# Expert slots of a fused encoder kernel laid out by token block, scattered once per two expert pairs

## The chip, the cores and the metric

The kernel runs on one core of a Trainium2 chip. The metric is the device time of one execution in microseconds (us); it is the median of three runs. The engines are named as in the profile: PE is TensorE (matmuls), PEld its weight loads, DVE is VectorE, ACT is ScalarE, POOL is GpSimd, and SP issues the DMAs.

## The reference, cut to what matters

Two layers work on x of 256 tokens by 1024 features, all in float32. Each layer has a token mixer and then a mixture of experts. The change touches the mixture of experts alone:

```
gate = one_hot(group) * (g_val * w_inner)         # (256 tokens, 16 experts), two nonzero in a row
hg = einsum('td,edf->tef', h, w_gate)             # w_gate, w_up: 16 x 1024 x 256
hu = einsum('td,edf->tef', h, w_up)
act = silu(hg) * hu * gate[..., None]
y = einsum('tef,efd->td', act, w_down)            # w_down: 16 x 256 x 1024
x = x + gt_f * y
```

The kernel doesn't compute all 256 x 16 products. Each expert has slots for the tokens that chose it: 32 (`CAP`) for each of the two blocks of 128 tokens. What does not fit goes through a loop, `extra`, which with these inputs runs for one pair of experts only (layer 1, pair 4).

## The kernel before, in words

The kernel writes out the order of the instructions of each engine by hand: they stand in program order, and an engine works strictly in that order. In each layer the experts are done in eight pairs, p = 0 to 7. One pair holds two experts of 64 slots, so 128 slots are the 128 partitions of every tile of that pair: 64 of the first expert (32 of block 0, 32 of block 1), then 64 of the second.

A pair goes through these steps:

- `gate_up` (L891): x of the slots (`xeT`) by the gate and up weights (`wgu`) gives `pgu`, 128 slots by 512. Two experts run side by side, each on 64 columns of the PE array, eight steps of the contraction, float32.
- `extra(p)` (L948): a branch on a counter; when it is zero, each engine jumps over the loop.
- `activate`: ACT takes the silu of the gate half (L906), DVE multiplies it with the up half and with `gs`, the gate weight of each slot (L907).
- `slots` for the next pair: POOL has written the selection matrix weighted by the gate (`sg`, L853); PE turns it (`pst`, two transposes, L897), ACT sums each row to `gs` (`junk`, L899, with an accumulator read behind it), DVE makes the 0/1 matrix `ST` (L901).
- for p < 4, `gather` of a part of x for the pairs 4 to 7: PE writes `pg` (L875), ACT (L881) and DVE (L883) scale it into `xeT`.
- half of `scatter` of the pair before (L942): `ST` by the two parts of its result (`yhi`, `ylo`), added to y in PSUM, token block 0; four matmuls.
- `turn`: PE transposes the activation (`pat`, L913), DVE copies it to SBUF (`atT`, L915).
- the other half of `scatter`, token block 1.
- `down` (L924): `pd`, two halves n of 512 features; behind each, DVE multiplies with the modulation (`yw`, L928), ACT rounds to `yhi` (L930), DVE takes the rest `ylo` (L932).

Pair 7 has no `slots`, and its result is scattered behind the loop (L1048 to L1051): the half n = 0 as yhi and ylo, the half n = 1 unsplit in float32 (`yw`). After it come the residual copies and the next layer, or in layer 1 the last norm and the store.

DMAs of weights are issued by SP up to two pairs ahead. Their order is the same in both kernels.

Of the kernel before, what the change touches and what calls it, by code (L numbers as in the profile page):

```python
# [7 lines left out]
F32 = mybir.dt.float32  # L8
F32R = mybir.dt.float32r
# [3 lines left out]
AF = mybir.ActivationFunctionType  # L13
# [4 lines left out]
P = 128  # L18
# [32 lines left out]
def encoder(ctx: ExitStack, tc: tile.TileContext, a: dict, out: bass.AP, dbg=None):  # L51
# [12 lines left out]
    def mid(name, shape=(P, D), dt=F32):  # L64
        return w4.tile(list(shape), dt, name=name, tag="w4")
# [49 lines left out]
    G.memset(ones, 1.0)  # L115
    zeros = const.tile([P, 1], BF16, name="zeros")
    G.memset(zeros, 0.0)
    sg = [const.tile([P, NB, 2, SL], F32, name=f"sg{i}") for i in range(2)]
    for t in sg:
        G.memset(t, 0.0)  # L120
# [632 lines left out]
    def experts(l):  # L753
# [140 lines left out]
        def slots(src, t=None):  # L894
# [6 lines left out]
            V.tensor_scalar(st, t, 0.0, None, op0=OP.is_gt)  # L901
            return gs_, st

        def activate(gate, up, gs_):
# [13 lines left out]
        def down(p, at, ts=(None, None), Y=None, last=False):
            hi, lo, w = Y or (mid("yhi", dt=F32R), mid("ylo", dt=F32R), mid("yw"))
            for n in range(2):  # L920
                t = bank("pd") if ts[n] is None else ts[n]
                for f in range(2):
                    for e in range(2):
                        mm(t[e * SL:(e + 1) * SL, :], at[:, f, e * SL:(e + 1) * SL],  # L924
                           WTS[l, p][2, e][:, f, n * 512:(n + 1) * 512], start=(f == 0), stop=(f == 1),
                           skip_group_check=True)
                sl = slice(n * 512, (n + 1) * 512)
                V.tensor_tensor(w[:, sl], t, gt[l, 1][:, sl], op=OP.mult)  # L928
                if not last or n == 0:
                    S.activation(hi[:, sl], w[:, sl], AF.Copy)  # L930
                if not last:
                    V.tensor_tensor(lo[:, sl], w[:, sl], hi[:, sl].bitcast(F32), op=OP.subtract)  # L932
            if last:
                sl = slice(0, 512)
                V.tensor_tensor(lo[:, sl], w[:, sl], hi[:, sl].bitcast(F32), op=OP.subtract)
            return hi, lo, w

        def scatter(st, Y, first, last, bs=(0, 1), ns=(0, 1)):
            for b in bs:
                for xi in range(2):  # L940
                    for n in ns:
                        mm(y[b][:, n * 512:(n + 1) * 512], st[:, b * P:(b + 1) * P],  # L942
                           Y[xi][:, n * 512:(n + 1) * 512], start=(first and xi == 0),
                           stop=(last and xi == 1), skip_group_check=True)

        def extra(p):
            v = nc.values_load(nx[0:1, p:p + 1], min_val=0, max_val=3)
            with tc.If(v > 0):  # L948
                rx = sm.tile([P, NB, 2], F32, name="rx", bufs=1)
                V.tensor_copy(rx, rk[:, :, 2 * p:2 * p + 2])  # L950
                with tc.For_i(0, v, 1):
                    V.tensor_scalar_add(rx, rx, -float(CAP))
                    gx = small("gx", (P, NB, 2, SL))
                    for b in range(NB):
                        V.tensor_tensor(sx[:, b, :, b * CAP:(b + 1) * CAP], iota[:, None, :].to_broadcast([P, 2, CAP]),
                                        rx[:, b, :, None].to_broadcast([P, 2, CAP]), op=OP.is_equal)
# [4 lines left out]
                    xr = mid("xr")  # L961
# [11 lines left out]
                    Y = mid("yhi", dt=F32R), mid("ylo", dt=F32R), mid("yw")  # L973
                    xe = Y[2].rearrange("p (d s) -> p d s", d=DC)
# [70 lines left out]
        st, Y = prev  # L1045
        for b in range(NB):
            s = st[:, b * P:(b + 1) * P]
            mm(y[b][:, 0:512], s, Y[0][:, 0:512], start=False, stop=False, skip_group_check=True)  # L1048
            mm(y[b][:, 512:D], s.bitcast(F32), Y[2][:, 512:D], start=False, stop=True,  # L1049
               skip_group_check=True)  # L1050
            mm(y[b][:, 0:512], s, Y[1][:, 0:512], start=False, stop=True, skip_group_check=True)  # L1051
# [110 lines left out]
```

## Time and profile before

| | before |
|---|---|
| median of 3 runs (lowest to highest) | 619.03 us (618.54 to 619.41) |
| the profiled execution's own time | 620.14 us |
| span of the profile, first to last instruction | 618.3 us |
| PE busy | 570.4 us, 92% of the span |
| DVE busy | 348.8 us, 56% |
| ACT busy | 212.5 us, 34% |
| mean granted clock of PE | 0.988 of full speed |

Busy shares are averages over the whole kernel. PE does little else than matmuls in the expert stages, from 179 to 298 us in layer 0 and from 477 to 610 us in layer 1; what the other engines set there are the short stretches between the end of a pair's `gate_up` and the start of its `down`. "Issue" as a releaser means that the engine waited for nothing that the profile shows.

### The profile page before, as it was taken

To read this page: it belongs to the slowest core of one execution; us is meant where nothing else is said; L and a number is where in the kernel's file an instruction comes from. 1 tells how busy PE (TensorE), PEld (TensorE's weight loads), DVE (VectorE), ACT (ScalarE), POOL (GpSimd) and SP (SyncE) were. 2 spreads that over 40 slices of the span, in tenths; PEclk is the share of its full clock that TensorE was granted. 3 is DMA by queue.
4 is the path that set the end of the run, shared out by engine and by line. 5 is a ranking of instruction groups with operands and counts; after the bars stand their busy time and mean duration, and the time that the engine had idled before them with its cause. 6 is when DMAs were issued, how large, how long until landed. Compare 5 with 4: busy or idle time off the path is not lost. (4 is left out here: it accounts for less than half of the span.)

```text
span 618.3 us, 8151 instructions
## 1 busy us (share of the span) xinstructions
PE 570.4 (92%) x3010; PEld 353.5 (57%) x3010; DVE 348.8 (56%) x670; ACT 212.5 (34%) x359; POOL 18.3 (3%) x56
## 2 busy tenths in 40 slices
PE   6998999999988999999899989999996999989994
PEld 4666874566444444343577789998864343453341
DVE  3988776542752333232788998899367233324223
ACT  6334345551433111111543744544335111112112
POOL 1000000000010000000000010000001000000000
PEclk9999999999997999999999989999999999999998
DMA  8999869999845999999998738698632799946911
GB/s 327 423 419 420 353 244 391 419 368 420 338 156 216 364 404 418 418 415 420 421 421 355 308 118 317 211 346 344 271 137 72 301 394 408 408 192 238 418 64 68
DMA packets 29188, 197.01 MB, mean 319 GB/s; under 512 B 3328, under 2 KB 3968, under 8 KB 7616
## 3 DMA queue, kind: packets, MB, share of 16 engines
q1 hardware_dynamic: 28832, 195.61, 79.3%
q8 instruction: 38, 0.62, 0.4%
q10 hardware_dynamic: 288, 0.52, 0.2%
q14 instruction: 30, 0.25, 0.1%
HBM read 195.08 MB, written 1.05 MB: 317 GB/s over the span
## 5 line engine op out<-in xcount | busy, mean ns | idle before, releaser
L891 PE MATMUL pgu<-wgu,xeT 128*64 128x512 f32 x512 | 112.7, 592 | 0.0
L891 PEld LDWEIGHTS pgu<-wgu,xeT 128*64 128x64 f32 x512 | 36.6, 137 | 72.3 <-issue 71.7
L219 DVE SCALAR_TENSOR_TENSOR wada<-wada,cact 128x1024 f32<-128x1024 f32 x56 | 66.2, 1218 | 0.7 <-ACT cact L168 0.7
L924 PE MATMUL pd<-wdn,atT 128*64 128x512 f32 x256 | 59.9, 611 | 1.7 <-DVE atT L915 1.7
L930 ACT ACTIVATE yhi<-yw 128x512 fp32r<-128x512 f32 x32 | 20.1, 629 | 94.1 <-DVE yw L928 94.1
L907 DVE SCALAR_TENSOR_TENSOR silu<-pgu,gs,silu 128x256 f32<-128x256 f32 x16 | 7.7, 484 | 75.4 <-ACT silu L906 75.4
L928 DVE TENSOR_TENSOR yw<-pd,gt 128x512 f32<-128x512 f32 x32 | 22.0, 688 | 41.2 <-PE pd L924 41.2
L714 PE MATMUL pu<-hhi,wlo 128*128 128x256 f32 x128 | 37.1, 290 | 2.3 <-DVE wlo L296 2.3
L924 PEld LDWEIGHTS pd<-wdn,atT 128*64 128x64 f32 x256 | 17.4, 140 | 35.8 <-issue 28.8
L714 PE MATMUL pu<-hhi,whi 128*128 128x256 f32 x128 | 37.8, 296 | 0.0
L714 PE MATMUL pu<-hlo,whi 128*128 128x256 f32 x128 | 36.8, 288 | 0.0
L932 DVE TENSOR_TENSOR ylo<-yw,yhi 128x512 fp32r<-128x512 f32 x30 | 20.8, 692 | 21.5 <-ACT yhi L930 13.9
L906 ACT ACTIVATE silu<-pgu 128x256 f32<-128x256 f32 x16 | 6.1, 384 | 74.3 <-PE pgu L891 72.3
L296 DVE TENSOR_TENSOR wlo<-win,whi 128x1024 fp32r<-128x1024 f32 x25 | 30.2, 1220 | 0.6 <-ACT whi L295 0.5
L714 PEld LDWEIGHTS pu<-hhi,wlo 128*128 128x128 f32 x128 | 25.2, 197 | 2.6 <-DVE wlo L296 2.5
L286 ACT ACTIVATE hhi<-hj,B 128x256 fp32r<-128x256 f32 x16 | 8.1, 509 | 52.6 <-DVE hj L278 26.3
L295 ACT ACTIVATE whi<-win 128x1024 fp32r<-128x1024 f32 x25 | 25.7, 1052 | 1.1 <-PE pu L714 1.1
L714 PEld LDWEIGHTS pu<-hhi,whi 128*128 128x128 f32 x128 | 25.3, 197 | 0.0
L714 PEld LDWEIGHTS pu<-hlo,whi 128*128 128x128 f32 x128 | 25.2, 197 | 0.0
L296 DVE TENSOR_TENSOR wlo<-bwo,whi 128x1024 fp32r<-128x1024 f32 x16 | 19.4, 1222 | 7.8 <-ACT whi L295 6.5
L942 PE MATMUL y<-yhi,ST 128*128 128x512 f32 x60 | 21.4, 430 | 0.6 <-PEq L948 0.3
L201 PE MATMUL pada<-wada,cz 128*32 128x512 f32 x160 | 20.7, 603 | 1.3 <-ACT VV L512 1.3
(263 smaller groups left out, 1058.9 us busy)
## 6 DMA issues: line engine op xcount, KB each, us to landing
wgu<-e_gu SPq DMA_DIRECT2D x64, 1024.0 KB, 9.7
wada<-w_ada SPq DMA_DIRECT2D x48, 1024.0 KB, 11.7
wdn<-e_dn SPq DMA_DIRECT2D x32, 1024.0 KB, 10.6
win<-w_in SPq DMA_DIRECT2D x16, 1024.0 KB, 12.9
bwo<-b_wo SPq DMA_DIRECT2D x8, 1024.0 KB, 4.9
wqk<-w_qk SPq DMA_DIRECT2D x8, 960.0 KB, 19.3
wv<-w_v SPq DMA_DIRECT2D x4, 960.0 KB, 19.4
wo<-w_o SPq DMA_DIRECT2D x3, 1024.0 KB, 7.4
```

The source lines that it names most:

```text
L201: mm(acc[l][q * 32:(q + 1) * 32, :], cz[:, k, e:e + 32], w[:, q * 512:(q + 1) * 512], start=(i == i0), stop=(i == i1), skip_group_check=True)
L219: V.scalar_tensor_tensor(w[:, h * D:(h + 1) * D], w[:, h * D:(h + 1) * D], 1.0, cact, op0=OP.mult, op1=OP.mult, accum_out=modc[l][:, c:c + 1])
L286: S.activation(hx[0][:, j, :], t, AF.Identity, bias=bb[:, j:j + 1])
L295: S.activation(hi[:m, :n], w, AF.Copy)
L296: V.tensor_tensor(lo[:m, :n], w, hi[:m, :n].bitcast(F32), op=OP.subtract)
L714: mm(pu[f // 2][:, f % 2, :], w_[:, k * 512 + f * P:k * 512 + (f + 1) * P], x_[:, kc, :], start=(kc == 0 and u == 0 and f % 2 == 0), stop= ...
L891: mm(t[e * SL:(e + 1) * SL, 0:n], x(k, e), WTS[l, p][e, k // 4][:, c:c + n], start=(k == 0), stop=(k == 7), skip_group_check=True)
L924: mm(t[e * SL:(e + 1) * SL, :], at[:, f, e * SL:(e + 1) * SL], WTS[l, p][2, e][:, f, n * 512:(n + 1) * 512], start=(f == 0), stop=(f == 1) ...
L928: V.tensor_tensor(w[:, sl], t, gt[l, 1][:, sl], op=OP.mult)
L930: S.activation(hi[:, sl], w[:, sl], AF.Copy)
L932: V.tensor_tensor(lo[:, sl], w[:, sl], hi[:, sl].bitcast(F32), op=OP.subtract)
L942: mm(y[b][:, n * 512:(n + 1) * 512], st[:, b * P:(b + 1) * P], Y[xi][:, n * 512:(n + 1) * 512], start=(first and xi == 0), stop=(last and ...
```

## The change

The slots of two pairs (a group r = p // 2) are laid out together. A pair's 128 partitions hold four tiles of 32 slots: in an even pair the tiles are expert 0 block 0, expert 1 block 0, expert 0 block 1, expert 1 block 1. In the odd pair the halves are swapped, block 1 first. So partitions 0 to 63 of the even pair and 64 to 127 of the odd pair belong to block 0. Their results are written into one tile per block (`Y[0][b]` and `Y[1][b]`, the yhi and ylo of block b), and one scatter with all 128 rows full serves both pairs.

- `gate_up_pair` and `down_pair` use 32-column tiles, four side by side: twice the matmuls, each with half the columns.
- `group` takes the place of `slots`: ahead of the loop and at p = 1, 3, 5 only; two transposes as before, but four ACT row sums of 64 rows by 128 in place of one of 128 by 256, because the two pairs need a `gs` each.
- the rounding `yhi` and the rest `ylo` are each done in two halves of 64 rows, since the rows go to different tiles. In pair 7 the n = 1 half is multiplied in two halves of 64 rows too.
- `scatter` of a group runs in full at p = 2 (group 0), in halves at p = 4 and 5 (group 1), 6 and 7 (group 2), and behind the loop (group 3). At p = 0, 1 and 3 none runs.
- `extra` uses the free tiles X[0], X[1] and one buffer `yx` for both halves n.

```diff
-        def weigh(p):
-            t = sg[p % 2]
-            es = slice(2 * p, 2 * p + 2)
-            for b in range(NB):
-                G.tensor_tensor(t[:, b, :, b * CAP:(b + 1) * CAP], sel[:, b, es, :].bitcast(F32),
-                                gf[:, b, es, None].to_broadcast([P, 2, CAP]), op=OP.mult)
+        def weigh(r):
+            t = sg[r % 2]
+            for b, i, e, n in ((0, 0, 4 * r, 4), (1, 2, 4 * r, 2), (1, 0, 4 * r + 2, 2)):
+                G.tensor_tensor(t[:, b, i:i + n, :], sel[:, b, e:e + n, :].bitcast(F32),
+                                gf[:, b, e:e + n, None].to_broadcast([P, n, CAP]), op=OP.mult)
             return t
...
+        def group(src):
+            t = bank("pst", (P, T))
+            for b in range(NB):
+                nc.tensor.transpose(t[:, b * P:(b + 1) * P], src[:, b].rearrange("p e c -> p (e c)"), ident)
+            gs = []
+            for o in range(2):
+                gs.append(sm.tile([P, 1], F32, name="gs", bufs=4))
+                for h in range(2):
+                    rs_, b = slice(h * SL, (h + 1) * SL), h ^ o
+                    S.activation(junk[rs_, :P], t[rs_, b * P:(b + 1) * P], AF.Copy, accum_out=gs[o][rs_, :])
+            st = small("ST", dt=F32R)
+            V.tensor_scalar(st, t, 0.0, None, op0=OP.is_gt)
+            return gs, st
+
+        def gate_up_pair(p, t):
+            for k in range(DC):
+                for q in range(4):
+                    e, b = q % 2, (q // 2) ^ (p % 2)
+                    c = (k % 4) * 512
+                    mm(t[q * CAP:(q + 1) * CAP, :],
+                       xeT[p // 4, k // 4][:, k % 4, 2 * (p % 4) + e, b * CAP:(b + 1) * CAP],
+                       WTS[l, p][e, k // 4][:, c:c + 512], start=(k == 0), stop=(k == 7), skip_group_check=True)
+
+        def down_pair(p, at, Y):
+            w = mid("yw") if p < 6 else Y[2]
+            for n in range(2):
+                t = bank("pd")
+                for f in range(2):
+                    for q in range(4):
+                        mm(t[q * CAP:(q + 1) * CAP, :], at[:, f, q * CAP:(q + 1) * CAP],
+                           WTS[l, p][2, q % 2][:, f, n * 512:(n + 1) * 512], start=(f == 0), stop=(f == 1),
+                           skip_group_check=True)
+                sl = slice(n * 512, (n + 1) * 512)
+                if p < 6 or n == 0:
+                    V.tensor_tensor(w[:, 0:512] if p > 5 else w[:, sl], t, gt[l, 1][:, sl], op=OP.mult)
+                for h in range(2):
+                    rs_, b = slice(h * SL, (h + 1) * SL), h ^ (p % 2)
+                    if p > 5 and n:
+                        V.tensor_tensor(Y[3][rs_, b, :], t[rs_, :], gt[l, 1][rs_, sl], op=OP.mult)
+                        continue
+                    S.activation(Y[0][b][rs_, sl], w[rs_, sl], AF.Copy)
+                    V.tensor_tensor(Y[1][b][rs_, sl], w[rs_, sl], Y[0][b][rs_, sl].bitcast(F32), op=OP.subtract)
...
-            act = activate(pgu[p][:, 0:T], pgu[p][:, T:2 * T], gs_)
-            if p + 1 < 8:
-                nxt = slots(sgn)
-                if p + 2 < 8:
-                    sgn = weigh(p + 2)
+            act = activate(pgu[p][:, 0:T], pgu[p][:, T:2 * T], grp[r][0][p % 2])
+            if r < 3:
+                if p % 2:
+                    grp[r + 1] = group(sgn)
+                else:
+                    sgn = weigh(r + 1)
             if p < 4:
                 gather(1, 2 * p, 2 * p + 2)
-            ada(A_E[l][p])
-            if prev:
-                scatter(*prev, False, False, (0,))
+            if p == 2 or p > 3:
+                scatter(grp[r - 1][1], Y[r - 1], (p % 2,))
             at = turn(act)
-            if prev:
-                scatter(*prev, False, False, (1,))
-            prev = (st, down(p, at, last=p == 7))
+            if p == 2:
+                scatter(grp[r - 1][1], Y[r - 1], (1,))
+            if p % 2 == 0:
+                Y[r] = outputs(p)
+            down_pair(p, at, Y[r])
```

How the instructions stand on the engines, at the three places that matter below. First PE in layer 0 at pair 3, from the transposes of the selection to the next pair's `gate_up`: before,

```order
L897 MATMUL pst<-cst,sg_98 128x128 x2
L875 MATMUL pg<-sel,xhi 128x8x32 x4
L875 MATMUL pg<-sel,xlo 128x8x32 x4
L942 MATMUL y<-yhi,ST 128x512 x2
L942 MATMUL y<-ylo,ST 128x512 x2
L913 MATMUL pat<-cst,silu 128x128 x2
L942 MATMUL y<-yhi,ST 128x512 x2
L942 MATMUL y<-ylo,ST 128x512 x2
L924 MATMUL pd<-wdn,atT 64x512 x8
L891 MATMUL pgu<-wgu,xeT 64x512 x16
```

and of the change:

```order
L904 MATMUL pst<-cst,sg_98 128x128 x2
L872 MATMUL pg<-sel,xhi 128x8x32 x4
L872 MATMUL pg<-sel,xlo 128x8x32 x4
L959 MATMUL pat<-cst,silu 128x128 x2
L930 MATMUL pd<-wdn,atT 32x512 x16
L920 MATMUL pgu<-wgu,xeT 32x512 x32
```

All eight scatter matmuls are gone from this place, the transposes stay, and `pd` and `pgu` have twice the matmuls.

Second, ACT at the same pair. Before:

```order
L906 ACTIVATE silu<-pgu 128x256
L899 ACTIVATE junk,gs<-pst 128x256
L881 ACTIVATE xeT<-pg,B_1192,G_1191 128x512
L930 ACTIVATE yhi<-yw 128x512 x2
```

and of the change:

```order
L952 ACTIVATE silu<-pgu 128x256
L910 ACTIVATE junk,gs<-pst 64x128 x4
L878 ACTIVATE xeT<-pg,B_1190,G_1189 128x512
L941 ACTIVATE yhi<-yw 64x512 x4
```

One row sum became four, and two roundings became four. On DVE the order around it is unchanged in such a pair (`silu`, `ST`, `xeT`, `atT`, in that order); in even pairs the `ST` is gone.

Third, DVE at pair 7 of layer 0, where the layer ends. Before:

```order
L907 SCALAR_TENSOR_TENSOR silu<-pgu,gs,silu 128x256
L915 COPY atT<-pat 128x256
L928 TENSOR_TENSOR yw<-pd,gt 128x512 x2
L935 TENSOR_TENSOR ylo<-yw,yhi 128x512
L296 TENSOR_TENSOR wlo<-win,whi 128x1024
L1059 COPY X_75<-y 128x512 x2
```

and of the change:

```order
L953 SCALAR_TENSOR_TENSOR silu<-pgu,gs,silu 128x256
L961 COPY atT<-pat 128x256
L935 TENSOR_TENSOR yw_3154<-pd,gt 128x512
L942 TENSOR_TENSOR ylo<-yw_3154,yhi 64x512 x2
L939 TENSOR_TENSOR yw<-pd,gt 64x512 x2
L294 TENSOR_TENSOR wlo<-win,whi 128x1024
L1099 COPY X_75<-y 128x512 x2
```

The multiplication of the second half (n = 1) moved from in front of `ylo` to behind it, and both are two instructions now.

## Rows read from the trace of the kernel before

**Rows 1.** Groups by line and form: busy us, mean ns | idle before it, releasers.

```profile
L891 PEld LDWEIGHTS pgu<-wgu,xeT 128*64 128x64 f32 x512 | 36.6, 137 | 72.3 <-issue 71.7 <-DMA wgu<-e_gu 0.6
```

**Rows 2.** Timeline (start, us, engine) of two PE stretches; 128*32 is the PE tile.

```profile
165.84 1.90 PE L201 MATMUL pada<-wada,cz 128*32 128x512 f32 x16
...
227.65 1.46 PE L891 MATMUL pgu<-wgu,xeT 128*64 128x512 f32 x6
```

**Rows 3.** Windows, gate_up to down: length; busy PE, PEld, DVE, ACT, POOL; clock; DMA.

```profile
186.15:194.09 7.94, 5.45 (x30) 4.09 (x29) 2.54 (x9) 3.89 (x7) 0.54 (x2) 0.76 0.45 165
205.90:209.97 4.07, 3.54 (x23) 2.73 (x21) 2.06 (x4) 1.63 (x4) 0.54 (x2) 1.00 0.71 254
220.31:224.17 3.86, 3.55 (x23) 2.73 (x21) 2.05 (x4) 1.64 (x4) 0.54 (x2) 1.00 0.99 365
...
248.95:251.84 2.89, 2.58 (x14) 1.77 (x13) 1.33 (x3) 0.86 (x3) 0.54 (x2) 1.00 1.00 411
262.18:265.37 3.19, 2.88 (x14) 1.77 (x13) 1.24 (x3) 0.86 (x3) 0.00 (x0) 1.00 0.99 408
...
288.95:291.53 2.58, 2.42 (x13) 1.57 (x11) 0.91 (x2) 0.38 (x1) 0.00 (x0) 1.00 0.96 394
...
483.77:486.94 3.17, 1.80 (x14) 1.37 (x12) 1.96 (x4) 1.63 (x4) 0.54 (x2) 1.00 0.55 158
497.29:501.15 3.86, 3.55 (x23) 2.73 (x21) 2.05 (x4) 1.64 (x4) 0.54 (x2) 1.00 0.95 337
511.49:516.71 5.22, 3.80 (x22) 2.78 (x20) 2.05 (x4) 1.64 (x4) 0.54 (x2) 1.00 1.00 403
```

**Rows 4.** Timeline of layer 0 pair 2, ACT and DVE and the copy.

```profile
220.95 0.48 DVE L907 SCALAR_TENSOR_TENSOR silu<-pgu,gs,silu 128x256 f32<-128x256 f32 x1 [4.87 <-ACT silu L906]
...
221.30 0.38 ACT L899 ACTIVATE junk<-pst 128x256 bf16<-128x256 f32 x1 [0.39 <-PE pst L897]
...
221.58 0.19 ACT L899 ACTIVATION_READ_ACCUMULATOR junk<-pst 128x1 f32 x1
221.81 0.42 DVE L901 TENSOR_SCALAR ST<-pst 128x256 fp32r<-128x256 f32 x1 [0.37 <-ACT junk L899]
...
222.15 0.80 DVE L883 TENSOR_SCALAR xeT<-pg,G,B 128x512 f32<-128x512 f32 x1
...
223.34 0.42 DVE L915 COPY atT<-pat 128x256 f32<-128x256 f32 x1 [0.39 <-PE pat L913]
```

**Rows 5.** Timeline of layer 0 pair 7, from the first scatter to the copy.

```profile
289.29 0.70 PE L942 MATMUL y<-yhi,ST 128*128 128x512 f32 x2 [0.16 <-PEq L948]
...
290.29 0.38 PE L913 MATMUL pat<-cst,silu 128*128 128x128 f32 x2
...
290.71 0.42 DVE L915 COPY atT<-pat 128x256 f32<-128x256 f32 x1 [0.64 <-PE pat L913]
```

**Rows 6.** Timeline of the end of layer 1's experts.

```profile
606.50 0.63 ACT L930 ACTIVATE yhi<-yw 128x512 fp32r<-128x512 f32 x1 [4.74 <-DVE yw L928]
...
607.43 0.69 DVE L928 TENSOR_TENSOR yw<-pd,gt 128x512 f32<-128x512 f32 x1 [1.03 <-PE pd L924]
608.04 0.68 DVE L935 TENSOR_TENSOR ylo<-yw,yhi 128x512 fp32r<-128x512 f32 x1
...
608.18 1.13 PE L1049 MATMUL y<-yw,ST 128*128 128x512 f32 x2 [0.36 <-DVE yw L928]
```

**Rows 7.** Groups by line and form, of half the rows and of few elements.

```profile
L296 DVE TENSOR_TENSOR wlo<-win,whi 128x1024 fp32r<-128x1024 f32 x25 | 30.2, 1220 | 0.6 <-ACT whi L295 0.5
L296 DVE TENSOR_TENSOR wlo<-wo,whi 64x1024 fp32r<-64x1024 f32 x1 | 1.2, 1219 | 4.6 <-ACT whi L295 4.6
L837 ACT ACTIVATE z<-z 128x10 f32<-128x10 f32 x2 | 0.4, 212 | 6.9 <-DVE z L836 6.9
```

**Rows 8.** Windows around the longest PE gap of layer 1 (columns as above).

```profile
365.30:367.70 2.40, 0.07 (x2) 0.05 (x1) 2.40 (x6) 2.31 (x3) 0.00 (x0) 1.00 0.00 0
367.70:371.10 3.40, 3.40 (x16) 3.40 (x17) 3.40 (x6) 0.00 (x0) 0.00 (x0) 0.50 0.33 92
```

More of the change, by code (lines that the diff above doesn't have):

```diff
@@ L117, in encoder @@
     G.memset(zeros, 0.0)
-    sg = [const.tile([P, NB, 2, SL], F32, name=f"sg{i}") for i in range(2)]
-    for t in sg:
-        G.memset(t, 0.0)
+    sg = [const.tile([P, NB, 4, CAP], F32, name=f"sg{i}") for i in range(2)]
     sx = const.tile([P, NB, 2, SL], F32R, name="sx")
@@ L904, in activate, with outputs @@
+        def outputs(p):
+            if p < 6:
+                return [[mid(n, dt=F32R) for b in range(NB)] for n in ("yhi", "ylo")]
+            hi, lo, w = mid("yhi", (P, NB, 512), F32R), mid("ylo", (P, NB, 512), F32R), mid("yw", (P, NB, 512))
+            return [[hi[:, b, :] for b in range(NB)], [lo[:, b, :] for b in range(NB)], mid("yw0", (P, 512)), w]
         def activate(gate, up, gs_):
@@ L916, in turn, with scatter @@
             return o
[L918 to L938, printed above, removed]
+        def scatter(st, Y, bs=(0, 1), ns=(0, 1)):
             for b in bs:
@@ L942, in scatter @@
                         mm(y[b][:, n * 512:(n + 1) * 512], st[:, b * P:(b + 1) * P],
-                           Y[xi][:, n * 512:(n + 1) * 512], start=(first and xi == 0),
-                           stop=(last and xi == 1), skip_group_check=True)
+                           Y[xi][b][:, n * 512:(n + 1) * 512], start=False, stop=False, skip_group_check=True)
         def extra(p):
@@ L972, in extra @@
                             S.activation(xr[:, n * 512:(n + 1) * 512], t, AF.Copy)
-                    Y = mid("yhi", dt=F32R), mid("ylo", dt=F32R), mid("yw")
-                    xe = Y[2].rearrange("p (d s) -> p d s", d=DC)
+                    w = X[1]
+                    xe = w.rearrange("p (d s) -> p d s", d=DC)
                     for h in range(2):
@@ L988, in extra @@
                     gate_up(p, (tx[2], tx[0]), lambda k, e: xe[:, k, e * SL:(e + 1) * SL])
-                    Y = down(p, turn(activate(tx[2][:, 0:T], tx[0][:, 0:T], gs_), tx[1]), (tx[0], tx[2]), Y)
+                    at = turn(activate(tx[2][:, 0:T], tx[0][:, 0:T], gs_), tx[1])
                     for n in range(2):
-                        scatter(st, Y, False, False, ns=(n,))
+                        t = tx[2 * n]
+                        for f in range(2):
+                            for e in range(2):
+                                mm(t[e * SL:(e + 1) * SL, :], at[:, f, e * SL:(e + 1) * SL],
+                                   WTS[l, p][2, e][:, f, n * 512:(n + 1) * 512], start=(f == 0), stop=(f == 1),
+                                   skip_group_check=True)
+                    yx = mid("yx", (P, 2, 512), F32R)
+                    for n in range(2):
+                        sl = slice(n * 512, (n + 1) * 512)
+                        V.tensor_tensor(w[:, sl], tx[2 * n], gt[l, 1][:, sl], op=OP.mult)
+                        S.activation(yx[:, 0, :], w[:, sl], AF.Copy)
+                        V.tensor_tensor(yx[:, 1, :], w[:, sl], yx[:, 0, :].bitcast(F32), op=OP.subtract)
+                        for b in range(NB):
+                            for i in range(2):
+                                mm(y[b][:, sl], st[:, b * P:(b + 1) * P], yx[:, i, :], start=False, stop=False,
+                                   skip_group_check=True)
         weights(l, 0, 0)
@@ L1007, in experts @@
         fill(len(fills))
-        nxt = slots(weigh(0))
-        sgn = weigh(1)
+        grp = {0: group(weigh(0))}
         ada(A_B[l][3])
-        prev = None
+        Y = {}
         for p in range(8):
-            gs_, st = nxt
+            r = p // 2
             pgu[p] = bank("pgu")
-            gate_up(p, [pgu[p]], lambda k, e: xeT[p // 4, k // 4][:, k % 4, 2 * (p % 4) + e, :])
+            gate_up_pair(p, pgu[p])
             weights(l, p + 1, 2)
@@ L1044, in experts @@
             in_split(0, 0)
-        st, Y = prev
+        st, Y = grp[3][1], Y[3]
         for b in range(NB):
             s = st[:, b * P:(b + 1) * P]
[L1048 to L1051, printed above, removed]
+            mm(y[b][:, 0:512], s, Y[0][b], start=False, stop=False, skip_group_check=True)
+            mm(y[b][:, 512:D], s.bitcast(F32), Y[3][:, b, :], start=False, stop=True, skip_group_check=True)
+            mm(y[b][:, 0:512], s, Y[1][b], start=False, stop=True, skip_group_check=True)
         (store if l else refresh)(y)
```

2 lines of the change are left out of this document (1 added, 1 removed).

## Prediction, made before the changed kernel ran

> **What bounds the kernel now.** I read the page's engine table first, then the groups by line, then the timeline of each expert pair. The groups say that PE never waits for weights to speak of in `gate_up`: of the weight loads' idle time 0.6 us in all is put down to a DMA, over 512 loads [rows 1]. So the matmul blocks are PE's own, and what can move is the stretch between a pair's `gate_up` and its `down`. Rows 3 has these stretches. With a gather and a scatter they last 3.86 us and PE is busy for 3.55 of them; without a gather 2.89; without a gather and a selection (pair 7) 2.58. PE fills them, so they look like PE work. But the timeline shows a second chain beside it: silu, multiplication, transposes (`pat`), copy (`atT`), `down`. In pair 7 the copy ends at 290.71 + 0.42 = 291.13 [rows 5], 2.18 after the stretch began at 288.95, and `down` starts at 2.58 [rows 3]. The scatter is cover for that chain, and taking it away gives at most 0.4 us there. That is the key to the forecast: what counts is the difference between two chains of nearly the same length.
>
> **The matmul blocks.** `gate_up` and `down` go from two 64-column tiles abreast to four 32-column tiles, with twice the instructions. The trace has both forms. Six matmuls on 64 columns, three rounds of two, last 1.46 us; sixteen on 32 columns, four rounds of four, last 1.90 [rows 2]. The fourth round adds 1.90 - 1.46 = 0.44 us, and with a round at 0.43 both are the same 0.60 us plus 0.43 for each further round. I cost this part at nothing. The bound on the other side is in the rivals.
> The Trainium skill (TensorE: Matmul & The Clock Gate, Part 3, "Measured speedup vs the span model") gives 2.38 times for three column tiles of M=32, so 0.79 a tile. By that, as an estimate, a round would be 0.43 / 0.79 = 0.54 us and the 24 rounds of each of 16 pairs +42 us, 661. The `pada` row contradicts it here.
>
> **Even pairs without a selection.** `pst`, `junk` and `ST` leave p = 0, 2, 4, 6. What `pst` and its start cost PE is the difference of two stretches that are otherwise alike: 2.89 - 2.58 = 0.31 us [rows 3].
> Pair 2 keeps gather and a full scatter, so PE fills it: -0.31 in each layer, -0.6.
> Pairs 4 and 6 keep only the first half of the scatter, which stands ahead of `pat`, as in pair 7 of before. Their chain is that of rows 5 up to the copy's end at 2.18, and `down` follows 0.06 later (the matmul behind 607.43 + 0.69 = 608.12 starts at 608.18 [rows 6]): 2.24. From 2.89 this is -0.65 for each of four pairs. In layer 1 pair 4 the taken `extra` now uses one buffer `yx` twice: the second rounding waits for matmuls on the first. That costs between nothing, if they are done by then, and 0.75, three scatter matmuls at a quarter of 290.29 - 289.29 = 1.00 us each [rows 5]; I take 0.3, since DVE's next multiplication covers about half. So -2.3 for the four.
> Pair 7 has the same chain: 2.24 for 2.58, -0.34 twice, -0.7.
> Pair 0: `ST` no longer stands ahead of `xeT` on DVE (0.34 from start to start [rows 4]), and `pst` is gone (0.31): between 0 and -0.65. In layer 1, whose stretch has PE busy for only 1.80 of 3.17 [rows 3], I take -0.5; in layer 0, whose 7.94 us also hold other work, -0.3. Together -0.8.
>
> **Odd pairs with a selection.** Here PE's scatter (p = 1, 3) or half of it (p = 5) goes, but the other chain grows. DVE works in order, and the copy stands behind `ST` and `xeT`; `ST` waits for the last row sum on ACT (0.04 us behind its read, 221.58 + 0.19 to 221.81 [rows 4]). Now there are four row sums. One of 128 elements costs: 0.38 for 256 elements [rows 4] against 0.212 for 10 [rows 7] is 0.7 ns an element, so 0.09 less for 128. Half the rows save nothing: 1219 ns on 64 rows, 1220 on 128 [rows 7], on DVE. From one row sum to the next I take 0.40 us: the 0.47 of rows 4 (221.30 to 221.77) less 0.09 is the lower bound, 0.38; the upper is 0.50, nothing saved and a little between them.
> The first starts 0.99 into the stretch (221.30 - 220.31). The last read ends at 0.99 + 3 x 0.40 + 0.38 = 2.57; `ST` at 2.61; `xeT` 0.34 later, 2.95; the copy 0.72 behind that (0.80 less the 0.08 by which two overlap on DVE: 221.81 + 0.42 against 222.15), 3.67 to 4.09; `down` at 4.15. Before: 4.07 in layer 0, 3.86 in layer 1 [rows 3]; pair 3 measures alike. So +0.1 and +0.3, each twice: +0.7.
> At p = 5 there is no `xeT`: copy 2.95 to 3.37, `down` at 3.43, for 3.19 in layer 0 (+0.24) and 2.89 in layer 1 (+0.54): +0.8.
> So removing eight scatter matmuls makes p = 1 and 3 no shorter at all.
> The Trainium skill (VectorE: DVE Perf Modes, "The TRN2 errata") says that the latency is paid for each instruction, and that many small tiles pay it each; it speaks against this cutting into halves. Rows 7 agree.
>
> **The roundings and the layer's end.** Six DVE and four ACT instructions behind `down` in place of four and two lie under the next `gate_up` (16 rounds of 0.43), in which both engines are idle. If that cover were gone it would be two DVE and two ACT instructions a pair, 2.5 us. At pair 7 there is no cover. Before, DVE does `yw` of n = 1 at 607.43, and PE's float32 matmul follows at 608.18 [rows 6]. Now the first `ylo` half starts when the first `yhi` half is done (606.50 + 0.63 + 0.04 = 607.17); the three behind it follow at DVE's pitch of 0.61 (607.43 to 608.04): the last multiplication from 609.00 to 609.69, and block 0 needs that one, since in an odd pair block 0 lies in the second half. PE then starts at 609.75, 1.57 later. PE's matmuls, the norm and the store follow in order. In layer 0 some 0.1 of it is absorbed, since DVE there had the next layer's `wlo` ahead of the copies. Together +3.0.
>
> **The sum.** -0.6 - 2.3 - 0.7 - 0.8 + 0.7 + 0.8 + 3.0 = +0.1 us on the profiled execution's 620.14. The median of before, 619.03, is lower by 1.1; I put the sum on the median: 619.1 us. Differences under 0.2% (1.24 us) count as the same, since the runs of before alone spread over 0.9.
>
> **The rivals.**
> *Forecast: no change.* Gains and losses of about 5 us each cancel. Unknown in it: the row sum's pitch (0.38 to 0.50: six stretches by three pitches by -0.02 to +0.10, -0.4 to +1.8), pair 0 (0 to -1.3 in all, +0.8 to -0.5 about the term), `extra` (-0.3 to +0.45), and the "issue" stall of layer 1 pair 2, whose stretch was 5.22 against 3.86 [rows 3]: 1.4 that may fall elsewhere, not at all, or twice with more instructions. Own range 617.3 to 621.0. Chance 0.46.
> *The clock falls in the odd pairs.* In p = 1 and 3 PE now has nothing between `pat` and `down`: `pat` follows the gather and ends near 2.1, so PE rests for some 2.0 us. Where PE had nearly nothing for 2.40 us, the granted clock was 0.50, 1.2 GHz, for the 3.40 us behind it [rows 8], which costs up to 1.7. The 1.37 us idle in layer 1's pair 0 left it at 1.00 [rows 3]. One fall is 620.8, all four 625.9. This is the rival on the other side: one fall already decides, together with nothing else. Chance 0.27, taken at 621.5.
> *PE is the bound and the rest follows.* If the copy's chain did not hold `down`, 32 of 62 scatter matmuls a layer at 0.25 us (8.0) and four of the eight selections' 0.31 (1.2) would go: 2 x 9.2 less the 3.0 of the tails, 603.6. For it: PE is busy for 3.55 of 3.86. Against: the copies' times in rows 4 and 5. Chance 0.04 in full; a part of it (odd pairs hide 1 us each, as when ACT's four sums run quicker than any row suggests, or the `issue` stall goes): 616.5, chance 0.19.
> *Four 32-column tiles do not run abreast with these operands.* If only two ran at a time, as now, the rounds would double: 24 x 0.43 x 16 pairs = +165 us, 784. Against it: rows 2. Chance 0.04, anywhere up to that.
>
> **How the numbers follow.** Faster by over 0.2%: the two PE-bound cases, 0.23, and a little of the forecast's lower edge: 0.26. Slower: the clock, 0.27, less the part of it that earlier gains hide, and the tiles 0.04, and the forecast's upper edge: 0.32. The same: 0.42. The range leaves out the full PE bound, the tiles, and the far ends of the clock case: 616.2 to 622.4.
>
> **What would show it.** In the trace after: rounds of `gate_up` and `down` still at 0.43 us. The stretch at p = 1 and 3 near 4.15 with the idle before `down` put down to DVE `atT`, and before `ST` to ACT `junk`; p = 5 near 3.43; p = 4, 6, 7 near 2.24; p = 2 near 3.55. At the ends, the float32 matmul 6.0 us behind the start of `down`, for 4.5 before. A granted clock below 1.00 behind p = 1 or 3 makes the clock case right; a copy that ends well ahead of 4.0 there makes the chain wrong; a round above 0.43 the tiles.

## The result, and the profile after

The changed kernel takes 629.7 us (median of four runs, 628.69 to 630.69), before 619.22 beside it: ratio 1.0159, 95% interval 1.0142 to 1.0176. It is 10.5 us slower; 619.1 and a range up to 622.4 were predicted. The profiled execution took 628.69 us, the shortest of the four; its span is 626.7 for 618.3, 8.4 us more. The other 2 us of the medians' difference lie in executions without a profile. The mean granted clock is 0.975 to 0.980 in its runs and 0.983 to 0.994 in those of before.

The stretches from the end of `gate_up` to the start of `down` in the changed kernel, as windows with the columns of rows 3; they answer to the rows there, in the order p = 0, 1, 2, 3, 4, 5, 6, 7 of layer 0, then p = 1, 2, 5 of layer 1:

```profile
186.46:194.10 7.64, 4.14 (x31) 3.11 (x28) 2.20 (x8) 3.53 (x5) 0.00 (x0) 1.00 0.42 150
206.08:210.74 4.66, 1.80 (x16) 1.41 (x13) 1.95 (x4) 3.05 (x10) 0.90 (x3) 1.00 0.71 262
222.73:226.47 3.74, 3.42 (x22) 2.56 (x19) 1.72 (x3) 1.16 (x2) 0.00 (x0) 1.00 0.98 340
236.79:241.43 4.64, 1.77 (x16) 1.41 (x13) 1.96 (x4) 3.05 (x10) 0.00 (x0) 1.00 1.00 397
253.42:256.37 2.95, 1.61 (x11) 0.96 (x7) 0.91 (x2) 0.39 (x1) 0.00 (x0) 1.00 1.01 417
266.68:270.56 3.88, 1.75 (x12) 1.13 (x8) 1.24 (x3) 2.28 (x9) 0.00 (x0) 1.00 1.02 420
280.88:283.16 2.28, 1.58 (x11) 0.92 (x7) 0.91 (x2) 0.38 (x1) 0.00 (x0) 1.00 1.03 417
293.48:295.74 2.26, 1.57 (x10) 0.91 (x6) 0.91 (x2) 0.38 (x1) 0.00 (x0) 1.00 1.03 424
...
501.24:505.90 4.66, 1.80 (x16) 1.41 (x13) 1.96 (x4) 3.05 (x10) 0.00 (x0) 0.93 0.94 360
517.57:521.27 3.70, 3.37 (x22) 2.54 (x18) 1.72 (x3) 1.16 (x2) 0.00 (x0) 1.00 0.92 328
...
581.28:585.29 4.01, 1.75 (x12) 1.24 (x9) 1.24 (x3) 2.27 (x9) 0.00 (x0) 1.00 1.01 419
```

Pairs 6 and 7 fell to 2.26 to 2.28, as forecast (2.24). Pairs 1 and 3 rose to 4.65, with PE busy for 1.8 us of it. The next windows are the `down` blocks behind them, from their start to the next `gate_up`: first pair 1 of layer 0, then pair 2 for comparison, then pair 3, and pairs 1 and 3 of layer 1. The column behind the busy times is the granted clock:

```profile
210.74:215.87 5.13, 5.13 (x33) 1.71 (x36) 1.63 (x3) 1.26 (x2) 0.00 (x0) 0.67 1.01 420
226.47:229.93 3.46, 3.46 (x34) 1.07 (x37) 0.71 (x2) 0.66 (x2) 0.00 (x0) 1.00 1.02 426
241.43:246.56 5.13, 5.13 (x33) 1.71 (x37) 1.66 (x3) 1.26 (x2) 0.00 (x0) 0.67 1.00 422
505.90:510.71 4.81, 4.80 (x32) 1.41 (x36) 0.77 (x2) 0.71 (x2) 0.00 (x0) 0.71 1.00 417
536.24:541.24 5.00, 5.00 (x33) 1.40 (x37) 0.77 (x2) 0.72 (x2) 0.00 (x0) 0.68 1.01 421
```

Behind each of the four stretches of 4.65 us the clock fell, and `down` took 4.81 to 5.13 us for 3.46: 6.2 us together. It isn't the DMA (the last two columns): pair 2, at 3.46 us, has the same share of 1.02. The weight loads show it as it happens. In layer 0 pair 1 the rounds start 0.43 us apart, and then 0.85 (timeline, PEld):

```profile
211.17 0.15 PEld L930 LDWEIGHTS pd<-wdn,atT 128*32 128x32 f32 x4 [0.27 <-issue]
211.60 0.16 PEld L930 LDWEIGHTS pd<-wdn,atT 128*32 128x32 f32 x4 [0.27 <-issue]
212.32 0.27 PEld L930 LDWEIGHTS pd<-wdn,atT 128*32 128x32 f32 x4 [0.56 <-issue]
213.17 0.27 PEld L930 LDWEIGHTS pd<-wdn,atT 128*32 128x32 f32 x4 [0.58 <-issue]
```

These four falls are new, but the clock falls in the kernel before too. The `down` of pair 0 of layer 0 is slow in both kernels, first before, then the change:

```profile
194.09:199.04 4.95, 4.95 (x18) 1.57 (x19) 0.81 (x2) 0.63 (x1) 0.00 (x0) 0.70 0.89 376
194.10:199.22 5.12, 5.12 (x32) 1.71 (x36) 1.24 (x2) 1.18 (x2) 0.00 (x0) 0.67 0.96 390
```

In before its stretch is at 0.76 as well (first line of rows 3), and PE's longest rest in it is 0.93 us.

Why the stretch of pair 1 is so long is in its timeline, which answers to rows 4 (the stretch begins at 206.08):

```profile
207.12 0.27 ACT L910 ACTIVATE junk<-pst 64x128 bf16<-64x128 f32 x1 [0.38 <-PE pst L904]
...
207.41 0.20 ACT L910 ACTIVATION_READ_ACCUMULATOR junk<-pst 64x1 f32 x1
207.63 0.27 ACT L910 ACTIVATE junk<-pst 64x128 bf16<-64x128 f32 x1
...
208.94 0.20 ACT L910 ACTIVATION_READ_ACCUMULATOR junk<-pst 64x1 f32 x1
...
209.17 0.42 DVE L912 TENSOR_SCALAR ST<-pst 128x256 fp32r<-128x256 f32 x1 [1.91 <-ACT junk L910]
209.51 0.80 DVE L880 TENSOR_SCALAR xeT<-pg,G,B 128x512 f32<-128x512 f32 x1
210.23 0.41 DVE L961 COPY atT<-pat 128x256 f32<-128x256 f32 x1
...
210.74 5.34 PE L930 MATMUL pd<-wdn,atT 128*32 128x512 f32 x32 [2.54 <-ACT xeT L878]
```

From one row sum to the next it is 0.51 us (207.12 to 207.63), not 0.40. DVE waits 1.91 us for the last of them, the copy comes behind `ST` and `xeT`, and PE rests for 2.54 us. (The releaser is named `xeT` on ACT, which ended at 209.94; the copy, which ended at 210.64, came last.)

At the end of layer 1, which answers to rows 6, the last multiplication and the matmul behind it; `down` had begun at 610.45:

```profile
615.22 1.39 DVE L939 TENSOR_TENSOR yw<-pd,gt 64x512 f32<-64x512 f32 x2
616.67 0.30 PEld L1090 LDWEIGHTS y<-yw,ST 128*128 128x128 f32 x2 [1.99 <-DVE yw L939]
```

That is 6.22 us behind the start of `down`, for 4.45 before.

### The profile page after: what moved, and what is told of

Read it like the earlier page. It is cut to its first block, busy times and chain, and to the rows that moved or that the text cites. A ratio compares the mean times of both kernels' runs of the same rounds, so it can differ in the third digit from the quotient of the medians.

```text
span 626.7 us, 9586 instructions
## 1 busy us (share of the span) xinstructions
PE 559.5 (89%) x3698; PEld 340.0 (54%) x3698; DVE 367.3 (59%) x692; ACT 236.3 (38%) x417; POOL 16.4 (3%) x46
## 5 line engine op out<-in xcount | busy, mean ns | idle before, releaser
L920 PE MATMUL pgu<-wgu,xeT 128*32 128x512 f32 x1024 | 113.0, 592 | 0.0
L930 PE MATMUL pd<-wdn,atT 128*32 128x512 f32 x512 | 66.2, 663 | 18.5 <-ACT xeT L878 11.0
L920 PEld LDWEIGHTS pgu<-wgu,xeT 128*32 128x32 f32 x1024 | 35.4, 110 | 73.5 <-issue 72.3
L941 ACT ACTIVATE yhi<-yw 64x512 fp32r<-64x512 f32 x56 | 35.2, 628 | 87.9 <-DVE yw L935 87.2
L942 DVE TENSOR_TENSOR ylo<-yw,yhi 64x512 fp32r<-64x512 f32 x56 | 38.5, 687 | 20.8 <-ACT yhi L941 20.0
L930 PEld LDWEIGHTS pd<-wdn,atT 128*32 128x32 f32 x512 | 18.1, 120 | 56.1 <-issue 34.5
L935 DVE TENSOR_TENSOR yw<-pd,gt 128x512 f32<-128x512 f32 x28 | 19.4, 692 | 39.8 <-PE pd L930 39.4
L587 PE MATMUL y<-whi,ghi 128*128 128x512 f32 x64 | 20.9, 398 | 0.0
```

Source lines behind the costliest of these rows:

```text
L587: mm(y[b][:, n * 512:(n + 1) * 512], x_[:m, c, b * P:(b + 1) * P], w_[:m, n * 512:(n + 1) * 512], start=(first and i == 0), stop=(last and ...
L920: mm(t[q * CAP:(q + 1) * CAP, :], xeT[p // 4, k // 4][:, k % 4, 2 * (p % 4) + e, b * CAP:(b + 1) * CAP], WTS[l, p][e, k // 4][:, c:c + 512 ...
L930: mm(t[q * CAP:(q + 1) * CAP, :], at[:, f, q * CAP:(q + 1) * CAP], WTS[l, p][2, q % 2][:, f, n * 512:(n + 1) * 512], start=(f == 0), stop= ...
L935: V.tensor_tensor(w[:, 0:512] if p > 5 else w[:, sl], t, gt[l, 1][:, sl], op=OP.mult)
L941: S.activation(Y[0][b][rs_, sl], w[rs_, sl], AF.Copy)
L942: V.tensor_tensor(Y[1][b][rs_, sl], w[rs_, sl], Y[0][b][rs_, sl].bitcast(F32), op=OP.subtract)
```

## The experiments

Ratios are to runs of before on the same chip, whose median was 620.4 (e1 to e4), 619.8 (e2b to e9) and 619.7 (e10 to e12).

**Work for PE in the rest.** e1 adds eight matmuls on zeros ahead of the transposes of the activation in pairs 1 and 3.

```diff
+            for _ in range(w):
+                mm(t, zeros.to_broadcast([P, P]), zeros.to_broadcast([P, 512]), start=True, stop=True)
...
-            at = turn(act)
+            at = turn(act, None, 8 if p in (1, 3) else 0)
```

> The changed kernel (629.7 us) with eight matmuls on zeros added on PE between the gather and the transposes of the activation in pairs 1 and 3, where PE rests; they compute nothing that is used. Theory A (PE's rest of 2.5 us lets the clock fall behind it): the stretches stay at 4.6 to 4.7 us, since DVE's chain ends them, the granted clock in the down behind them is 1.00 and down falls from 5.0 to 5.1 back to 3.46 us, four times about 1.5: 623.0 to 624.5 us. Theory B (four 32-column tiles run slow in these downs, whatever PE did before): unchanged, 629 to 631 us.

Measured: 625.76 us (621.4 to 626.95), ratio 1.0098, 1.0081 to 1.0115. In the profiled execution, the one of 621.4, the stretches keep their length and none of the four `down` blocks behind them is slow (stretch and `down` of pair 1, then of pair 3, layer 0; in layer 1 both `down` take 3.43 us as well):

```profile
203.87:208.53 4.66, 3.50 (x23) 2.21 (x21) 1.96 (x4) 3.05 (x10) 0.90 (x3) 1.00 0.80 287
208.53:211.96 3.43, 3.43 (x32) 1.26 (x36) 0.75 (x2) 0.70 (x2) 0.00 (x0) 1.00 1.03 432
232.86:237.50 4.64, 3.47 (x23) 2.21 (x21) 1.96 (x4) 3.05 (x10) 0.00 (x0) 1.00 1.01 420
237.50:240.93 3.43, 3.43 (x32) 1.25 (x36) 0.75 (x2) 0.70 (x2) 0.00 (x0) 1.00 1.01 425
```

So the clock follows the rest. The median gained 4 us and not 6. The execution of 621.4 is a favourable one: the `down` of pair 0 of layer 0 ran at full clock too (3.43 us), and its mean clock is 0.994. In the other four it was 0.981 to 0.988, in the runs of before beside them 0.983 to 0.988. So clock falls remain in them; whether any is one of the four, their times don't tell.

**The tiles alone, in the pairs and in the loop.** e2 cuts every 64-column tile of the kernel before in two, in `gate_up` and `down`, which `extra` uses as well.

> The kernel before (619.2 us) with gate_up and down on four 32-column tiles, each 64-column tile cut in two; nothing else differs. Theory A (the tiles cost nothing, the clock falls by PE's rest): rounds of 0.43 us, 618.2 to 620.5 us. Theory B (the tiles are slow where the weights stream in): some downs at 5 us and 623 to 627 us; if the rounds are longer everywhere, far more.

Measured: 656.85 us, ratio 1.058, 1.0559 to 1.0601. Neither theory had that. The rounds are 0.43 us; what is long are PE's waits behind the branch over `extra` (waits of PE put down to PEq, its own sequencer: us in total, times, longest; first before, then e2):

```profile
PE pst L897 <- PEq L948: 4.3, 13, 0.5
```

```profile
PE pst L898 <- PEq L949: 30.8, 13, 4.1
```

The edit had doubled the instructions of the loop too, which is jumped over in fifteen of sixteen pairs. Two more runs take it apart.

**The tiles alone, in the pairs only.** e2b leaves the loop as it was.

```diff
+        def gate_up32(p, t):
+            for k in range(DC):
+                for q in range(4):
+                    e, h = q // 2, q % 2
...
+                    mm(t[q * CAP:(q + 1) * CAP, :],
+                       xeT[p // 4, k // 4][:, k % 4, 2 * (p % 4) + e, h * CAP:(h + 1) * CAP],
```

> The kernel before (619 to 620 us) with gate_up and down of the eight pairs on four 32-column tiles; the loop of extra is left as it was (the run e2_before32 had doubled its code too). Theory A (the tiles cost nothing by themselves): rounds of 0.43 us and stretches as before, 619 to 621.5 us. Theory B (the tiles are what is slow): over 625 us. Theory D (it is code: the waits of 4 us at the branch over extra in e2_before32 come from the length of code jumped over, and go when that is short again): at most two or three waits above 0.5 us at the branch, against 16 us of them in layer 0 there.

Measured: 622.46 us, ratio 1.0045, 1.0027 to 1.0063: 2.7 us, 1 more than theory A gave, with the clock at 0.984 to 0.993. Rounds are 0.43 us (20 matmuls in 2.33). In its trace some stretches are longer than before, at other places than in before, as pair 1 of layer 1 and pair 5 of layer 0:

```profile
497.88:503.10 5.22, 3.54 (x25) 2.81 (x21) 2.05 (x4) 1.64 (x4) 0.55 (x2) 1.00 0.92 345
...
262.13:266.02 3.89, 2.60 (x16) 1.78 (x13) 1.24 (x3) 0.86 (x3) 0.00 (x0) 1.00 0.99 413
```

PE is no busier in them than in the like ones [rows 3]. So the tiles cost nothing as matmuls. The 2.7 us are waits, of PE for its sequencer (4.9 us at twelve places behind the branch, for 4.3 at thirteen) and for other engines; that they come with the doubled instructions is argued and not shown.

**The loop alone.** e12 has 32-column tiles in the loop only; the pairs execute what before executes.

> The kernel before with 32-column tiles only in the loop of extra, which is jumped over in fifteen of sixteen pairs; what the pairs themselves execute is unchanged. Theory D (a longer jump costs waits for code): PE waits of about 4 us behind the branch as in e2_before32, 640 to 655 us. If e2_before32 was slow for its pairs' tiles together with the loop, or for another reason: 619 to 622 us.

Measured: 635.73 us, ratio 1.0254, 1.0232 to 1.0277. Below the range of theory D, but 16 us for code that runs in one pair. The waits behind the branch:

```profile
PE pst L898 <- PEq L950: 17.1, 13, 3.5
```

17.1 us for 4.3. The Trainium skill (Runtime: NRT & Kernel Launch, "Instruction fetch mechanics") says that a taken branch whose target isn't among the code pages at hand has to fetch it first; these waits agree. They are 12.8 us of the 16.

**The branch taken out.** e10 and e11 keep `extra` in layer 1 pair 4 alone, in the changed kernel and in before.

```diff
-            extra(p)
+            if (l, p) == (1, 4):
+                extra(p)
```

> The changed kernel with the branch over extra left out in the fifteen pairs in which it isn't taken with these inputs (the loop stays in layer 1 pair 4). Theory D (part of the loss is waiting at the branch for code): the PE waits put down to the branch, 4.9 us in all behind the fifteen, go, -3 to -5 us against its ratio to before (1.016), 624.5 to 627 us where before is at 619.5. Theory A alone: the odd stretches end by DVE's chain, which starts at ACT's silu behind the branch, so they keep 4.6 us and the clock still falls four times; only pairs 2, 4, 6 and 7 gain, 0.2 each: 627.5 to 629 us.

> The same edit on the kernel before: 4.6 us of PE waits stand behind the branch, and PE fills these stretches, so it gains about all of them but what ACT's silu holds: -2 to -5 us, 614.5 to 617.5 us where before is at 619.5. With e10 it tells how much of the 1.016 belongs to the branch.

Measured: e10 625.14 us, ratio 1.0069, 1.0049 to 1.0089, 5.6 us less than the changed kernel by the ratios, as theory D has it; e11 611.8 us, ratio 0.9872, 0.9849 to 0.9896, 7.9 less than before, beyond what was expected. Without the branch the changed kernel is slower by 13.3 us and not by 10.5, so the branch doesn't explain the loss; it is a cost of its own in both. The 7.9 us are not the branch's waits alone: in the profiled execution of e11 the stall of layer 1 pair 2 is gone (3.51 us for 5.22) and the `down` of layer 0 pair 0 ran at full clock (3.48 for 4.95). In e10 the clock still falls (stretch and `down` of pair 1):

```profile
205.46:210.02 4.56, 1.74 (x16) 1.40 (x13) 1.96 (x4) 3.05 (x10) 0.90 (x3) 1.00 1.00 424
210.02:215.15 5.13, 5.13 (x33) 1.71 (x37) 0.94 (x2) 0.88 (x2) 0.00 (x0) 0.67 1.02 415
```

**The rest on the old tiles.** e7 is the kernel before without the scatter in pairs 1 and 3 and with three more row sums there.

```diff
+            for i in range(more):
+                S.activation(junk[0:SL, :P], t[0:SL, 0:P], AF.Copy, accum_out=gx_[0:SL, :])
...
-                nxt = slots(sgn)
+                nxt = slots(sgn, None, 3 if p in (1, 3) else 0)
...
-            if prev:
+            if prev and p not in (1, 3):
```

> The kernel before, on its 64-column tiles, made to rest as the changed one does: at pairs 1 and 3 the scatter is left out (so y lacks two pairs' results) and three more row sums of 64 x 128 stand behind the one there is. Theory A: the stretch is about 4.6 us with PE at rest for 2.4 to 2.5 of it, the clock falls to half in the four downs behind, which take 5.0 to 5.1 us for 3.48: +6.2 for the clock and +0.6 to +0.8 for each stretch, 627 to 630 us. Theory B (the slow downs come with the 32-column tiles): downs at 3.48 us, 621.5 to 623.5 us.

Measured: 624.39 us (620.6 to 625.99), ratio 1.0071, 1.0051 to 1.0091. Less than expected, because the stretches are 4.25 to 4.44 us for 4.6, and one of the four downs kept its clock; the others took 5.15 to 5.16 us. Pair 1 of layer 0, which kept it, and pair 1 of layer 1, which didn't:

```profile
207.36:211.80 4.44, 1.75 (x14) 1.40 (x13) 1.96 (x4) 2.62 (x10) 0.54 (x2) 1.00 0.71 247
211.80:215.25 3.45, 3.45 (x16) 1.41 (x18) 0.78 (x2) 0.63 (x1) 0.00 (x0) 1.00 1.02 430
...
499.08:503.34 4.26, 1.76 (x15) 1.40 (x13) 1.95 (x4) 2.62 (x10) 0.55 (x2) 1.00 0.85 327
503.34:508.49 5.15, 5.15 (x16) 1.91 (x18) 0.99 (x2) 0.63 (x1) 0.00 (x0) 0.67 0.99 393
```

A slow `down` of 5.15 us on 64-column tiles: it comes with PE's rest and not with the new tiles, so theory B falls. The rest ahead of `down` was 2.19 us at this place and at two where the clock fell; at the fourth, pair 3 of layer 0, it is in two parts of 0.77 and 1.17 us, and the clock fell too. So the length of one rest doesn't settle it.

The stretches are shorter than 4.6 us because the added row sums, of the same form as the changed kernel's, follow one another faster (pair 3, layer 0):

```profile
237.84 0.27 ACT L903 ACTIVATE junk<-pst 64x128 bf16<-64x128 f32 x1
238.01 0.19 ACT L903 ACTIVATION_READ_ACCUMULATOR junk<-pst 64x1 f32 x1
238.23 0.27 ACT L903 ACTIVATE junk<-pst 64x128 bf16<-64x128 f32 x1
```

The read starts 0.17 us behind the start of its sum, before the sum has ended, and the next sum 0.39 us behind it, for 0.29 and 0.51 in the changed kernel.

**One row sum in place of four.** e8 uses one sum of 128 by 256 for both pairs; it leaves out the right gate weights.

> The changed kernel with one row sum of 128 x 256 in each group in place of four of 64 x 128, used for both pairs (the gate weights are then wrong: sums over both blocks). Theory A: the last read ends 1.5 us earlier, stretches of pairs 1 and 3 fall to 3.1 us and pair 5 to about 2.4; PE rests 1.0 us and the clock stays at 1.00: -9 for the stretches of both layers, -6 for the clock, 614 to 617 us. If the row sums were not what the stretch waits for: above 626 us.

Measured: 618.61 us, ratio 0.9981, 0.9965 to 0.9996; expected 614 to 617. Stretch and `down` of pair 1:

```profile
207.31:210.49 3.18, 1.78 (x16) 1.38 (x13) 1.96 (x4) 1.75 (x4) 0.90 (x3) 1.00 0.62 188
210.49:213.95 3.46, 3.46 (x33) 1.07 (x36) 0.77 (x2) 0.72 (x2) 0.00 (x0) 1.00 1.05 436
```

4.66 became 3.18 and the clock held. By the ratios 11 us go, as much as the whole loss of 10.5. The 2 us missing from the expectation are at other places, as pair 5 of layer 1, where the stretch is 3.83 us and should be 2.6, as it is in layer 0, and the `down` of pair 0 of layer 0, 6.17 us at a clock of 0.55.

**The selection behind `down`.** e3 moves `group` there, so that row sums and `ST` lie under the next `gate_up`.

```diff
-            if r < 3:
-                if p % 2:
-                    grp[r + 1] = group(sgn)
-                else:
-                    sgn = weigh(r + 1)
+            if r < 3 and p % 2 == 0:
+                sgn = weigh(r + 1)
...
             down_pair(p, at, Y[r])
+            if r < 3 and p % 2:
+                grp[r + 1] = group(sgn)
```

> The changed kernel with the selection of the next two pairs (transposes, four row sums, ST) moved behind the odd pair's down, under the next gate_up. Theory A: stretches of pairs 1 and 3 fall from 4.65 to 2.6 to 2.9 us (-7.2 for four), pair 5 from 3.9 to 2.3 (-3.3 for two), the clock stays at 1.00 (-6.2), the transposes now stand between down and gate_up (six times 0.2 to 0.3): 613 to 616 us. Theory B (the slow downs belong to the tiles): -9 only, 619 to 622 us. Theory C (the row sums cost time wherever they stand, since silu and yhi wait behind them on ACT): above 622 us.

Measured: 619.1 us, ratio 0.9976, 0.9963 to 0.9989; expected 613 to 616 where before is at 619.2. The stretches fell as theory A has it and the clock held there (pair 1, layer 0), but other places gave back some 4 us, as the `down` of pair 0 of layer 0 (6.18 us for 5.12 in the changed kernel) and that of pair 5 of layer 1, at full clock:

```profile
207.92:210.68 2.76, 1.61 (x15) 1.24 (x12) 1.62 (x3) 1.16 (x2) 0.00 (x0) 1.00 0.59 157
210.68:214.62 3.94, 3.94 (x35) 1.30 (x35) 1.27 (x2) 1.21 (x2) 0.00 (x0) 1.00 1.00 424
194.88:201.06 6.18, 6.18 (x32) 1.69 (x36) 1.75 (x3) 1.26 (x2) 0.00 (x0) 0.55 0.78 326
...
573.43:579.00 5.57, 4.98 (x35) 1.26 (x35) 1.26 (x2) 1.21 (x2) 0.00 (x0) 1.00 1.01 419
```

**The order at the layer's end.** e4 puts the multiplication of n = 1 ahead of `ylo` in pair 7, the rows for block 0 first.

```diff
+                for h in ((1, 0) if p == 7 else (0, 1)):
...
+                    if p < 7 and not (p == 6 and n) or p == 7 and n:
+                        ls = slice(0, 512) if p == 7 else sl
+                        V.tensor_tensor(Y[1][b][rs_, ls], w[rs_, ls], Y[0][b][rs_, ls].bitcast(F32), op=OP.subtract)
```

> The changed kernel with DVE's order at pair 7 changed: of the half n = 1 the multiplication of the rows that block 0 needs first comes ahead of the remainders ylo. Theory A: the float32 matmul starts 4.5 us behind the start of down again, for 6.2; -1.7 us in layer 1; in layer 0 the same, or nothing if the next layer's waits absorb it: 626.0 to 628.2 us. Rival: the end of the layers is held by the norm and the copies and not by this chain: 629 to 630.5 us.

Measured: 626.82 us (624.97 to 629.45), ratio 1.0095, 1.0072 to 1.0118. The float32 matmul starts 4.46 us behind the start of `down`, 613.12:

```profile
617.58 0.70 PE L1092 MATMUL y<-yw,ST 128*128 128x512 f32 x1 [0.38 <-DVE yw L939]
```

The spread of its runs is too wide to say whether layer 0 gained as well as layer 1.

**The two together.** e9 has this order, row sums and `ST` behind `down`, and the transposes of the selection between those of the activation and `down`, where PE rests.

```diff
+            pst = flip(sgn) if r < 3 and p % 2 else None
             down_pair(p, at, Y[r])
+            if r < 3 and p % 2:
+                grp[r + 1] = sums_of(pst)
```

> The changed kernel with the transposes of the selection between the transposes of the activation and down, where PE rests anyway, the row sums and ST behind down's roundings, and pair 7's order on DVE as in e4_tail. Theory A: stretches of pairs 1 and 3 at 2.8 us, pair 5 at 2.4 to 2.6, down to gate_up 3.46 us without the 0.48 that e3_late_group paid six times, and 1.7 us less at the end: 3 to 5 us below e3_late_group's ratio to before (0.9976), so 613.5 to 617 us where before is at 619.5. Rival (the transposes don't fit into the rest, or instruction waits and the clock take it back): 618 to 620 us.

Measured: 612.94 us (612.19 to 613.42), ratio 0.9893, 0.9871 to 0.9916, just below the range expected. It leaves nothing out and beats both kernels. Pair 1 of layer 0:

```profile
205.67:208.38 2.71, 1.83 (x16) 1.42 (x13) 1.62 (x3) 1.16 (x2) 0.58 (x2) 1.00 0.48 127
208.38:211.84 3.46, 3.46 (x33) 1.07 (x37) 0.77 (x2) 0.72 (x2) 0.32 (x2) 1.00 1.00 424
```

## Why the prediction was wrong

The sum, term by term, against the two profiled executions (span 618.3 to 626.7, +8.4); the clock's term is that of the four `down` blocks behind pairs 1 and 3:

| term | forecast | in the trace |
|---|---|---|
| pair 0 | -0.8 | -0.7, with the clock in layer 0 at 0.76 before and 1.00 after |
| pair 2 | -0.6 | -0.3, and -1.4 as the stall of before is gone |
| pairs 4 and 6 | -2.3 | -1.4 |
| pair 7 | -0.7 | -0.6 |
| pairs 1 and 3 | +0.7 | +2.7 |
| pair 5 | +0.8 | +1.8 |
| the layers' ends | +3.0 | +1.9 |
| the clock | none | +6.2 |
| other places | none | +0.2 |

**The step that failed** is the choice among the rivals: "The clock falls in the odd pairs" was there, with its place, its mechanism and "all four 625.9", and it was given 0.27 at one fall, while the forecast kept the clock at 1.00. It fell behind all four in the profiled execution, 6.2 us, and the mean clocks of the other runs are as low. e1 (work in the rest), e7 (rest on the old tiles), e3 and e8 (rest taken away) show that the rest is the cause. The prediction had a rest with a fall behind it (2.40 us, PE busy 0.07) and one without (1.37 us), and with "some 2.0" between them it gave no row for the harmless side. It read the 7.94 us of layer 0 pair 0 in rows 3 for their length and not for their clock of 0.76, the other fall that its rows show.

**A mis-sized term beside it** is the row sum's pitch: "I take 0.40 us" between 0.38 and 0.50 is 0.51 us. The instruction itself did get shorter, 0.27 for 0.38, but the read of the accumulator starts behind its end (0.29 behind its start, 207.12 to 207.41), where in rows 4 it started before the end (0.28 of 0.38). In e7 sums of the same form have a pitch of 0.39, so 0.40 was a fair reading of the form; why the read waits in the changed kernel stays open. e8, with one sum of 128 rows, has the late read too (208.33 to 208.73). Three pitches are 0.33 us too little in each of six stretches; with 0.16 more for the first one's start and the last one's end the copy came at 4.15 and not at 3.67, and PE rested for 2.54 us and not for "some 2.0". This made 3 us of direct loss. The fall doesn't hang on it: e7, with rests of about 2.2 us, fell at three of four places.

**Right:** that the scatter was cover and that its removal shortens nothing where DVE's chain is longer; the even pairs (2.26 to 2.28 at pairs 6 and 7 for 2.24); the matmul rounds at 0.43 us; the pitch of DVE at the end (1.77 later for 1.57). **Right, but taken back or covered:** pair 4 of layer 0 lost its gain to a wait of 0.82 us at the branch. At the end of layer 0 the later start of 1.75 us shows as 0.2 us at layer 1's first `gate_up`. The fall of the clock in rows 8 did not come in this execution (0.94 in 360 to 390 before, 1.00 in 364 to 394 after), which is worth the 1.7 us of that row; that the two belong together is argued and not shown.

**Wrong by being left out:** the tiles "at nothing" cost no matmul time, but with them the kernel before is 2.7 us slower by waits (e2b). That number doesn't stand beside the others in the table, since these waits are in the stretches already. What each of them waits for stays open.

## What to carry to other kernels

Work that fills an engine beside a chain of other engines is free to keep: before it is removed, write down when the chain itself would end, and what the engine does in the rest that appears. A rest of PE can be priced twice, for itself and for the slower clock behind it. No single length decided the second price here (2.19 us fell at two places and held at one), so the rival with the falls needs a full place in the range; look for falls in the clock column of every stretch of before. Serial row sums cost by the instruction (e8: three fewer, 1.5 us), so a selection that needs four belongs where it is covered: with row sums and `ST` under the next matmul block and the order at the layer's end mended, the same change gained 1.1% in place of losing 1.6%.

## What was not expected of the hardware

- A row sum on ACT with an accumulator read, 64 rows of 128 elements, took 0.51 us from start to start in the changed kernel and 0.39 in e7, although the instruction itself is 0.27 us in both: the read starts behind the sum's end in the one and before it in the other. What makes the difference is open.
- Twice the matmuls in a loop that is jumped over cost 16 us (e12), 17.1 us of PE waits at thirteen places for 4.3; and leaving the branch out gains 7.9 us in before (e11), where its visible PE waits are 4.6; a stall and a clock fall elsewhere went with them.
- Whether the clock falls behind a rest of 2.19 us differs between places of one execution (e7). In e9 a rest of 2.30 us in pair 5 of layer 1 left it at 1.00 (`down` behind it 3.43 us), and in before it fell in pair 0 of layer 0, where no rest is over 0.93 us.
